# A step table in place of counted slots in the attention stage of a two-mixer step, with the multiplications of the values shared out anew

## The chip, the cores and the metric

The kernel runs on one core of one Trainium2 chip. The time is the device time of one execution in microseconds; the figure given is the median of several runs. An execution taken by the hardware profiler comes with its span (first to last instruction on the core) and with its own time, which includes what lies around the span.

Five engines work beside each other, each through its own instruction stream in order: TensorE (PE; PEld is its weight load), VectorE (DVE), ScalarE (ACT), GpSimd (POOL) and SyncE (SP, which here issues most DMAs). An instruction waits for semaphores of others, and what stands behind it on its engine waits with it. PSUM has eight banks of 128 x 512 float32.

## What is computed

One layer with two attention mixers side by side: mixer A attends to all latent tokens, mixer B to a window of 128 to each side with a sink logit; both see 128 cached context tokens. Each branch is multiplied by a SiLU gate, and both go through one output projection.

```python
h = rmsnorm(xs, norm_gain) * (1.0 + scale) + shift
q_a, k_a, v_a, g_a, q_b, k_b, v_b, g_b = project(h, w_in, ...)
...
o_a = global_attn_latent(q_a, k_a, v_a, cache_k_a, cache_v_a)
o_b = window_attn_latent(q_b, k_b, v_b, cache_k_b, cache_v_b, sink_b)
xs = xs + gate * merge_out(o_a, g_a, o_b, g_b, w_out)
...
def merge_out(o_a, g_a, o_b, g_b, w_out):
    return jnp.concatenate([o_a * jax.nn.silu(g_a), o_b * jax.nn.silu(g_b)], axis=-1) @ w_out
```

There are 1024 latent tokens (8 tiles of 128) and 128 prompt tokens (one tile, t = 0), which attend only to themselves. D is 1024; each mixer has 8 heads of 64 in 2 key/value groups. Everything is float32; matrix products are made of high and low parts (`F32R`), so that one product in the text is two or three matmuls in the code.

## The kernel before

**Stages.** To about 300 us: adaLN modulation and normalisation, then the projections (gates, queries, keys and values). Queries go to DRAM (`q_dram`, high and low halves), SiLU gates to `g_dram`, keys and values stay in SBUF. The attention stage follows, on which the change acts.

**Units and pairs.** A unit is (t, m, g): a token tile, a mixer (m = 0 is A, m = 1 is B) and a key/value group. `units` lists them tile by tile, A before B, so units 2k and 2k+1 are a pair with the same t and g. There are 18 pairs: 0 to 15 for the latent tiles, 16 and 17 for the prompt. A unit holds four heads of 128 queries.

**An A unit** (m = 0):
- `max_items`: twelve times a matmul `pmx` (L932, one head by three key blocks, a bank of tag A) and VectorE's maximum over it (L933). `finish` reduces them to `m_nat`, negated (L943, L946); `transpose` turns this 128 x 4 tile on TensorE (`ptm`, L951, a bank of tag A) and VectorE multiplies it into four rows of the query tile `qb` (L952), so that the second score matmul subtracts the maximum.
- `scores`: per key block two matmuls into `st` (L1206, L1207, a bank of tag B), ScalarE's exponential `pe` (L1208), and GpSimd's addition into `acc` (L1215), for the sums.
- `values`: per block a product into `pv` (L1228, a bank of tag C; four instructions, because the two halves of the columns go separately and each is float32), at the end one of `acc` by ones for the sums.

**A B unit** (m = 1):
- `weight_items`: per head two matmuls into `sn` (L989, L990, tag A), VectorE's masked minimum `nm` (L993), ScalarE's exponential `pen` (L979). Then small steps: GpSimd `ex` (L1011), ScalarE `sinks` (L1022), GpSimd `total` (L1025), VectorE's reciprocal `inv` (L1028). `turned` transposes `inv` (`pti`, L1040, tag A), `put` copies it (L1044) and sends it to DRAM, `rows` reads it back broadcast over partitions.
- `scores`: four transposes of `pen` into `st` (L1202, tag B) and a copy by ScalarE (L1203) per block. `values` as above.

**After the values.** For A, `inverse` makes reciprocal sums `rs` on ScalarE (L1245, L1246). GpSimd multiplies the gate tile `sgl` by the reciprocals (A at L1248, B at L1036). `gated`: VectorE multiplies `pv` by this `sgl` into `of` (L1254). `parts`: ScalarE copies it to the high part `ogh` (L1264), GpSimd subtracts for the low part `ogl` (L1267). `out_items` are the output matmuls `po` (L1305, banks D and E), 24 per pair, which fill TensorE during later pairs; VectorE adds the residual and SP stores.

**Banks.** A, B and C have two each, D and E one. A bank of a tag is used again when the readers of the one before the last are done.

**Order.** The program is written in one order, and `in_order` at the end keeps each engine to it. That order came from slots: one slot per score block, 13 for a middle pair. In each slot the loop at the end of `hybrid_step` ran `tick()` (what `later(n, f)` had put n slots ahead), one score block, the due steps (offsets MX_AT, NAT_AT, ENDS, EX_AT, ROWS_AT), six of the `late` products (the last gate columns, `late_product`, L1137) in each of the first four slots, and output matmuls at a rate of OUTRATE a slot out of a queue `outq`. Steps of the end of a unit were set relative to when its values were issued.

Of the kernel before, what the change touches and what calls it, by code (L numbers as in the profile page):

```python
# [1 line left out]

# [32 lines left out]
KS = (0, 1, 4, 5, 2, 3, 6, 7)  # L35
PL_DVE = (4,)
LAG = 2
LEAD = 4
# [4 lines left out]
NAT_AT = (0, 1, 2, 3)  # L43
NAT_FIRST = (0, 1, 2, 3)
MX_AT = (-4, -3, -2, -2, -1, 4, 5, 5, 7, 7, 8, 8)
MX_FIRST = (0, 1, 2, 3, 3, 4, 4, 5, 6, 7, 7, 8)
MX_LEAD = 3
LAST_END = (1, 3, 5, 7)
SPLIT_LAG = 2

LATE = (6, 6, 6, 6)
LATE_PUT = 9
LATE_LAG = 1
# [4 lines left out]
WO_LATE = {12: 9, 13: 10, 11: 21, 15: 21, 14: 24}  # L58

WO_STEPS = ((0, 4, 4), (1, 5, 5), (2, 6), (3, 7), (4, 8, 6), (5, 9), (6, 11), (7, 12, 10), (8, 12), (9, 13), (10, 14))  # L60
TURN = 2
QUERY_AT = (0, 2, 3, 6)
PAD = 2
# [11 lines left out]
LOADLEAD = 5  # L75
OUTRATE = 2.0
# [4 lines left out]
GATE_LATE = 2  # L81
ENDS = ((1, 3, 4), (1, 2, 3, 6))
QTS = 5
PROMPT_LEAD = 4
PROMPT_PV = "CCAC"
PROMPT_PL = ()
LOW_DVE = (-2, -1)
PROMPT_EX = (1, 2)
PROMPT_RATE = 4

HELD = 2
END_RATE = 2.5
EX_AT = (2, 2, 5)
ROWS_AT = (1, 1, 4, 6)
# [13 lines left out]
GROUP = (1, 2, 4)  # L108

# [21 lines left out]
def hybrid_step(ctx, tc, x_prompt, x_sample, cache_k_a, cache_v_a, cache_k_b, cache_v_b,  # L131
# [15 lines left out]
    agenda = {}  # L147
    now = [0]

    def later(n, f):  # L150

        agenda.setdefault(now[0] + n, []).append(f)

    def tick():
        now[0] += 1
        for f in agenda.pop(now[0], ()):
            f()
# [615 lines left out]
    with tc.tile_pool(name="kt", bufs=2) as kt:  # L773
# [94 lines left out]
        def tick_now():  # L868
            for f in agenda.pop(now[0], ()):
                f()  # L870

# [42 lines left out]

    def max_items(i):
# [4 lines left out]
        def item(h, b):  # L920
            if h == 0 and b == 0:
                mxtile[i] = qs.tile([P, 4, 3], F32, tag="mx", name=f"mx{i}", bufs=3)
            mx = mxtile[i]
            lhs = qtile[i][:, P * h : P * h + P]
# [6 lines left out]
            else:  # L931
                nc.tensor.matmul(pm[:, 0:384], lhs, kha[:, g, 3 * b : 3 * b + 3, :], start=True, stop=True)  # L932
                nc.vector.tensor_reduce(mx[:, h, b : b + 1], pm[:, 0:384], axis=AX.X, op=ALU.max)  # L933

        def finish():
# [4 lines left out]
            mn = m_nat[i // 2 % 2]  # L940
            if t > 0:
# [5 lines left out]
            later(TURN, transpose)  # L947

        def transpose():
            pt = bank("A", f"ptm{i}")  # L950
            nc.tensor.transpose(pt[0:4, 0:P].bitcast(F32R), m_nat[i // 2 % 2], ident_r)  # L951
            nc.vector.tensor_tensor(qbtile[i][64:68, :].rearrange("p (h n) -> p h n", h=4),  # L952
                                    pt[0:4, 0:P].unsqueeze(1).to_broadcast([4, 4, P]),
# [7 lines left out]
    def weight_items(i):  # L961

        t, m, g = units[i]
        v = {}

# [12 lines left out]
        def exp(h, s, scale):  # L978
            nc.scalar.activation(penat[i][:, h], s, AF.Exp, bias=v["nm"][:, h : h + 1], scale=scale,  # L979
                                 accum_out=v["sum"][:, h : h + 1])  # L980

        def item(h):
            p0, p1_ = window(t)
            n = P * (p1_ - p0)
            if h == 0:
                first(n)
# [231 lines left out]
    def values(i, made, first, last):  # L1218
# [39 lines left out]
        def parts():  # L1258
            while held[0] == NOG:
                outq.pop(0)()  # L1260
# [186 lines left out]
```

## Time and profile before

| what | value |
|---|---|
| median of 3 runs | 694.82 us (693.71 to 695.19) |
| profiled execution, own time | 694.89 us |
| its span | 693.0 us |
| mean granted TensorE clock | 0.994 |
| TensorE matmuls | 3896 |
| VectorE / ScalarE / GpSimd instructions | 857 / 692 / 340 |

The views that the next sections use: the page (busy time and share of each engine); busy time by stage, whose rows give a stretch, its length, the busy time of PE, PEld, DVE, ACT and POOL with their instruction counts, the granted clock, the DMA share and GB/s; the timeline, whose rows give the start, the duration, engine, line, operation, what is written from what, and a count where like instructions were merged, with the engine's idle time before it and who ended it in brackets; the groups of instructions by line (count, then busy us and mean ns, then idle us before and who ended it); the waits (total us, times, longest). A matmul's bar is longer than the time until the next one may start.

### The profile page before, as it was taken

How to read it: one execution, taken by the hardware profiler on the slowest of the kernel's cores; microseconds unless marked ns; L12 is line 12 of the kernel's file. 1: busy time of each engine (PE TensorE's matmuls, PEld its weight loads, DVE VectorE, ACT ScalarE, POOL GpSimd, SP SyncE). 2: the span in 40 equal slices, each digit the busy share in tenths (PEclk: the TensorE clock that was granted, in tenths of full speed). 3: DMA queues.
4: the chain of work that ended last, by engine and by line, in shares of the span. 5: the costliest groups of instructions: out<-in, count | busy, mean ns of one | idle time of the engine just before them, and what ended most of it. 6: DMA issues, size and time to landing. Idle time of an engine off the chain costs nothing.

```text
span 693.0 us, 10923 instructions
## 1 busy us (share of the span) xinstructions
PE 675.0 (97%) x3896; PEld 522.8 (75%) x3896; DVE 374.3 (54%) x857; ACT 309.0 (45%) x692; POOL 323.3 (47%) x340
## 2 busy tenths in 40 slices
PE   6999999999999999998999999999999999999997
PEld 3688988878788788985667777777777777777666
DVE  3565237875684772535446455455455563645343
ACT  4555411412243452456445445555456445545450
POOL 3466023332322140657575457545664566446730
PEclk9999999999999999999899999999999999999999
DMA  8960283339436015533122122212221212112323
GB/s 339 413 255 21 109 303 77 78 92 285 133 88 191 8 62 161 165 105 108 58 82 71 54 85 68 92 54 69 70 84 47 91 61 78 55 55 68 122 61 122
DMA packets 53446, 78.65 MB, mean 113 GB/s; under 512 B 6848, under 2 KB 25728, under 8 KB 52368
## 3 DMA queue, kind: packets, MB, share of 16 engines
q1 hardware_dynamic: 45360, 66.28, 28.4%
q10 hardware_dynamic: 8032, 11.68, 6.3%
q8 instruction: 31, 0.51, 0.3%
q14 instruction: 23, 0.19, 0.1%
HBM read 58.72 MB, written 19.21 MB: 112 GB/s over the span
## 4 chain that ended last, share of the span: by engine, by line
PE 87%; DMA 4%; DVE 3%; ACT 2%; issue 1%; POOL 1%; ACTq 1%; SPq 1%; DVEq 0%; POOLq 0%
PE pv L1228 14%; PE po L1305 14%; PE st L1206 5%; PE pmx L932 5%; PE st L1207 4%; PE pq L279 4%; PE pq L280 4%; PE pq L278 4%; PE st L1202 4%; PE pg L288 3%; PE pg L292 3%; PE pg L293 3%; PE pk L279 2%; PE pk L280 2%; PE pk L278 2%; DMA wm<-in_w_mod_ss_dram 2%
## 5 line engine op out<-in xcount | busy, mean ns | idle before, releaser
L1215 POOL TENSOR_TENSOR acc<-acc,pe 128x512 f32<-128x512 f32 x112 | 143.5, 1281 | 37.8 <-ACT pe L1208 35.4
L933 DVE TENSOR_REDUCE mx<-pmx 128x1 f32<-128x384 f32 x192 | 101.7, 554 | 103.8 <-PE pmx L932 101.5
L1208 ACT ACTIVATE pe<-st 128x512 f32<-128x512 f32 x146 | 85.4, 596 | 89.8 <-PE st L1207 89.6
L1228 PE MATMUL pv<-pe,v_all 128*64 128x256 f32 x832 | 101.6, 387 | 0.0
L1228 PEld LDWEIGHTS pv<-pe,v_all 128*64 128x64 f32 x832 | 57.3, 138 | 38.3 <-issue 8.4
L993 DVE CUSTOM_DVE_ANT_0 sn<-sn,mask,nsink 128x512 f32<-128x512 f32 (+1 forms) x64 | 46.3, 724 | 68.6 <-PE sn L990 67.9
L1305 PE MATMUL po<-wo,ogh 128*128 128x512 f32 (+1 forms) x224 | 75.8, 390 | 0.0
L197 POOL TENSOR_TENSOR rs_q<-ms_q,mhalf 128x8 f32<-128x8 f32 x18 | 34.8, 1931 | 80.8 <-DVE ms_q L195 80.8
L932 PE MATMUL pmx<-kha,qt 128*128 128x384 f32 x192 | 63.3, 376 | 3.7 <-ACT pen L979 3.1
L1215 POOL TENSOR_TENSOR acc<-pe,pe 128x512 f32<-128x512 f32 x16 | 20.4, 1276 | 96.2 <-ACT pe L1208 73.9
L1206 PE MATMUL st<-qt,kha 128*128 128x512 f32 x144 | 61.4, 426 | 1.2 <-ACT pe L1208 1.1
L979 ACT ACTIVATE pen<-sn,nm 128x512 f32<-128x512 f32 (+2 forms) x72 | 45.3, 631 | 31.4 <-DVE nm L993 28.6
L1207 PE MATMUL st<-qb,kla 68*128 68x512 f32 x144 | 57.2, 397 | 0.0
L1203 ACT COPY pe<-st 128x512 f32<-128x512 f32 x62 | 36.4, 587 | 32.9 <-PE st L1202 32.9
L932 PEld LDWEIGHTS pmx<-kha,qt 128*128 128x128 f32 x192 | 34.9, 192 | 12.8 <-ACT pen L979 7.7
L1305 PEld LDWEIGHTS po<-wo,ogh 128*128 128x128 f32 x224 | 41.5, 190 | 3.5
L1305 PE MATMUL po<-wo,ogl 128*128 128x512 f32 (+1 forms) x112 | 43.6, 389 | 0.0
L1206 PEld LDWEIGHTS st<-qt,kha 128*128 128x128 f32 x144 | 27.2, 189 | 20.9 <-issue 8.5
L1202 PE MATMUL st<-ident_r,pen 128*128 128x128 f32 x248 | 37.5, 274 | 1.1 <-DVE pen L1030 1.1
L441 POOL TENSOR_TENSOR h<-hf,h 128x256 fp32r<-128x256 f32 (+2 forms) x33 | 28.0, 862 | 20.7 <-DVE h L440 20.7
L1202 PEld LDWEIGHTS st<-ident_r,pen 128*128 128x128 f32 x248 | 29.2, 141 | 7.5 <-ACT ogh L1264 1.5
L675 ACT ACTIVATE sqq<-pq 128x512 f32<-128x512 f32 x18 | 10.8, 599 | 53.3 <-DMA qd<-qo0q 15.6
(235 smaller groups left out, 1506.9 us busy)
## 6 DMA issues: line engine op xcount, KB each, us to landing
qt<-qd SPq DMA_DIRECT2D x36, 256.0 KB
wm<-in_w_mod_ss_dram SPq DMA_DIRECT2D x8, 1024.0 KB
qd<-qo0q ACTq DMA_DIRECT2D x36, 128.0 KB
qd<-qo1q ACTq DMA_DIRECT2D x36, 128.0 KB
sgl<-gd SPq DMA_DIRECT2D x36, 128.0 KB
out_dram<-yt SPq DMA_DIRECT2D x17, 256.0 KB
xn<-in_x_sample_dram SPq DMA_DIRECT2D x8, 512.0 KB
wg<-in_w_mod_g_dram SPq DMA_DIRECT2D x4, 1024.0 KB
```

What stands on the lines that cost most here:

```text
L278: nc.tensor.matmul(out, h_at(0, i, k, tok), w.hi[k], start=(k == 0), stop=False)
L932: nc.tensor.matmul(pm[:, 0:384], lhs, kha[:, g, 3 * b : 3 * b + 3, :], start=True, stop=True)
L933: nc.vector.tensor_reduce(mx[:, h, b : b + 1], pm[:, 0:384], axis=AX.X, op=ALU.max)
L979: nc.scalar.activation(penat[i][:, h], s, AF.Exp, bias=v["nm"][:, h : h + 1], scale=scale, accum_out=v["sum"][:, h : h + 1])
L993: nc.vector.tensor_tensor_reduce(s, s, mask[:, m0 : m0 + n], -1.0, nsink[:, 4 * g + h : 4 * g + h + 1], op0=ALU.add, op1=ALU.min, accum_ou ...
L1202: nc.tensor.transpose(s[:, P * h : P * h + P], penat[i][:, h, o : o + P], ident_r.bitcast(F32))
L1206: nc.tensor.matmul(s, kh, qtile[i], start=True, stop=False)
L1207: nc.tensor.matmul(s, kl, qbtile[i], start=False, stop=True)
L1208: nc.scalar.activation(pe, s, AF.Exp)
L1215: nc.gpsimd.tensor_tensor(acc[i], first, pe, op=ALU.add)
L1228: nc.tensor.matmul(pv[HD * s : HD * s + HD, o : o + 256].rearrange("p (c n) -> p c n", c=2), lhs, r[:, :, s, :], start=start, stop=stop)
L1305: nc.tensor.matmul(po[c], x, wo_parts[KT * n + k][lo][:, q], start=(k == KS[0] and p == 0), stop=(k == KS[-1] and p == 2))
```

## The change

- All offsets of slots are replaced by a table `STEPS`: every step of a pair has a place (a real number) relative to the pair's start, pairs are `PAIR = 13` apart, and `OTHER` has places of their own for pairs 0, 15, 16 and 17. `agenda` becomes a heap, and the stage runs everything in order of its place. The places make an order only; nothing waits for a clock. Output matmuls have places too (`po`), so the queue `outq` with its rate is gone.
- The first value products of an A unit (`v1`) come after eight score blocks, before after six.
- `gated`: VectorE multiplies `pv` by the reciprocals (`rs` or `rows`), GpSimd then multiplies `of` by the gates, before the copy `ogh`. The two GpSimd multiplications of `sgl` go. The prompt's B units, whose weights are already divided, are multiplied by the gates on VectorE as before.
- `ptm` and `pti` become riders: if the next `pmx` comes within `mt_wait` or `nt_wait` steps, they are written to columns 384 to 511 of its bank, just ahead of it; otherwise to a bank of their own.
- `KS`, the order of the eight input tiles of the output matmuls, starts with the B mixer.
- The 24 late products are spread by `LATE`; loads (`qa`, `qb` query tiles, `wa`, `wb` gate tiles, `nr` rows) have places in the table.

```diff
-KS = (0, 1, 4, 5, 2, 3, 6, 7)
+KS = (4, 5, 0, 1, 6, 7, 2, 3)
...
+PAIR = 13
+STEPS = {'qa': -19.96,
+         'mx': (-16.71, -16.71, -15.16, -14.85, -13.67, -8.98, -7.88, -7.77, -6.05, -5.92, -5.82, -5.62),
+         'mf': -2.8,
+         'mt': -1.53,
+         'mt_wait': 0.01,
+         'sa': (0.08, 0.59, 1.46, 2.33, 3.28, 4.04, 6.45, 6.92, 9.09),
+         'qb': -2.9,
+         'nm': (0.23, 1.26, 1.81, 3.27),
+         'nx': (0.83, 1.26, 2.62, 3.27),
+         'nf': 3.45,
+         'ns': 4.53,
+         'nn': 5.14,
+         'nd': 6.55,
+         'nt': 7.13,
+         'nt_wait': 1.08,
+         'np': -0.21,
+         'nr': 13.0,
+         'sb': (8.81, 10.61, 11.27, 11.69),
+         'v1': 7.15,
+         'v2': 14.7,
+         'ea': 15.2,
+         'ga': 16.66,
+         'ha': 17.94,
+         'la': 19.03,
+         'gb': 16.29,
+         'hb': 17.86,
+         'lb': 18.69,
+         'po': (21.51, 22.08, 22.28, 23.38, 23.52, 23.64, 23.67, 24.08, 24.17, 24.18, 24.99, 25.69, 25.98, 26.08, 26.94, 28.37, 29.56, 29.77, 29.93, 30.27, 30.4, 31.0, 31.45, 31.48),
+         'wa': -5.73,
+         'wb': -8.28}
...
+LATE = ((-0.86, 2), (-0.61, 1), (-0.17, 3), (-0.16, 1), (1.64, 3), (2.52, 1), (2.92, 1), (2.97, 1), (3.46, 5), (5.27, 3), (5.31, 1), (6.78, 1), (6.89, 1))
...
+    def of_pair(i, name, f, k=None):
+        w = when(i, name)
+        w = PAIR * (i // 2) + (w if k is None else w[k])
+        if zero:
+            post(zero[0] + w, f)
+        else:
+            soon.append((w, f))
+
+    def beside_maxima(i, name, f, wait):
+
+        r = name, f
+        riders.append(r)
+        later(wait, lambda: r in riders and (riders.remove(r), f(bank("A", name)[0:4, 0:P])))
...
             else:
+                if riders:
+                    riders.pop(0)[1](pm[0:4, 384:512])
                 nc.tensor.matmul(pm[:, 0:384], lhs, kha[:, g, 3 * b : 3 * b + 3, :], start=True, stop=True)
...
-            later(TURN, transpose)
...
+            of_pair(i, "mt", lambda: beside_maxima(i, f"ptm{i}", transpose, when(i, "mt_wait")))
...
-            later(ROWS_AT[0], turned)
-            later(ROWS_AT[1], put)
-            later(ROWS_AT[2], rows)
-            later(ROWS_AT[3], lambda: nc.gpsimd.tensor_tensor(sgl[i], sgl[i], v["rows"], op=ALU.mult))
...
+            of_pair(i, "nt", lambda: beside_maxima(i, f"pti{i}", turned, when(i, "nt_wait")))
...
-            sg = sgl[i]
-            later(1, lambda: nc.gpsimd.tensor_tensor(sg, sg, rs.rearrange("p (c n) -> p c n", c=2), op=ALU.mult))
+            inv[i] = rs.rearrange("p (c n) -> p c n", c=2)
...
-            nc.vector.tensor_tensor(of, pv[:, 0:256].rearrange("p (c n) -> p c n", c=2), sgl.pop(i), op=ALU.mult)
-            later(GATE_LATE, lambda: load_gate(i + 4))
...
+            whole = t == 0 and m == 1
+            by = sg if whole else inv.pop(i)
+            nc.vector.tensor_tensor(of, pv[:, 0:256].rearrange("p (c n) -> p c n", c=2), by, op=ALU.mult)
+            if not whole:
+                nc.gpsimd.tensor_tensor(of, of, sg, op=ALU.mult)
             v["of"] = of
...
+        for name, f in zip("eglh", (inverse, gated, low, parts)):
+            if m == 0 or name != "e":
+                of_pair(i, name + "ab"[m], f)
         if m == 1:
-            later(ENDS[m][3], lambda: outq.extend(out_items(t, g)))
+            for k, f in enumerate(out_items(t, g)):
+                of_pair(i, "po", f, k)
...
+    while agenda:
+        n, _, f = heappop(agenda)
+        now[0] = max(now[0], n)
         f()
```

In the table a name stands for: `mx` a maximum, `mf` and `mt` the end of the maxima and ptm, `sa` and `sb` a score block of A and of B, `nm` and `nx` a head's window scores and its exponential, `nf`, `ns`, `nn`, `nd` the small steps ex, sinks, total and reciprocal, `nt`, `np`, `nr` pti, put and rows, `v1` and `v2` the value products, `e`, `g`, `h`, `l` with a or b the steps inverse, gated, parts (ogh) and low (ogl). When a step is posted after its place has passed, it runs next.

341 lines of the change are left out of this document (214 added, 127 removed).

## Prediction

> **What bounds the kernel now.** I read the page first, then the busy time by stage.
>
> ```profile
> span 693.0 us, 10923 instructions
> PE 675.0 (97%) x3896; PEld 522.8 (75%) x3896; DVE 374.3 (54%) x857; ACT 309.0 (45%) x692; POOL 323.3 (47%) x340
> ...
> 300.00:323.00 23.00, 22.56 (x138) 17.07 (x137) 8.78 (x22) 16.07 (x36) 14.94 (x14) 1.00 0.29 92
> 323.00:354.00 31.00, 27.37 (x136) 18.89 (x135) 14.94 (x35) 15.72 (x38) 20.65 (x22) 0.89 0.25 82
> 354.00:627.00 273.00, 272.87 (x1634) 200.06 (x1633) 148.00 (x337) 141.17 (x326) 159.12 (x168) 1.00 0.22 69
> 627.00:675.00 48.00, 46.02 (x292) 33.05 (x292) 20.13 (x45) 24.20 (x68) 25.98 (x33) 1.00 0.29 88
> ```
>
> TensorE sets the time. The change acts only after 300 us, in the attention stage, and removes no matmul; so it can gain only what TensorE loses there to waits and to a lower clock (third number from the right). The busy column hides short waits, since a matmul's bar is longer than its share of the pipe. The distance from one start to the next shows them. TensorE's timeline in a middle pair:
>
> ```profile
> 432.08 0.60 PE L1202 MATMUL st<-ident_r,pen 128*128 128x128 f32 x4
> 432.44 0.60 PE L932 MATMUL pmx<-kha,qt 128*128 128x384 f32 x2
> 432.87 0.39 PE L1305 MATMUL po<-wo,ogl 128*128 128x512 f32 x1
> 433.10 0.40 PE L1305 MATMUL po<-wo,ogh 128*128 128x512 f32 x1
> 433.51 0.22 PE L951 MATMUL ptm<-ident_r,m_nat 128*4 128x128 f32 x1
> ...
> 438.07 0.60 PE L1228 MATMUL pv<-acc,ones 128*64 128x256 f32 x4
> 438.51 1.68 PE L1228 MATMUL pv<-pe,v_all 128*64 128x256 f32 x14
> ...
> 444.33 0.39 PE L1206 MATMUL st<-qt,kha 128*128 128x512 f32 x1
> 444.56 0.39 PE L1207 MATMUL st<-qb,kla 68*128 68x512 f32 x1
> 444.82 0.62 PE L932 MATMUL pmx<-kha,qt 128*128 128x384 f32 x2
> 445.28 0.39 PE L1305 MATMUL po<-wo_big,ogh 128*128 128x512 f32 x1
> ...
> L951 PE MATMUL ptm<-ident_r,m_nat x12: 223/224/227, 365.2 to 615.6; 128*4 128x128 f32 x12
> PEld ptm L951 <- DVE mx L933: 5.3, 12, 0.5
> PEld pmx L932 <- ACT pen L979: 3.3, 11, 0.3
> ```
>
> A 512-column matmul costs 0.23 us (432.87 to 433.10, 444.33 to 444.56). Four transposes and two maxima take 432.08 to 432.87, 0.79: I take 0.11 a transpose and 0.175 a maximum. A value product (four instructions) takes 0.44 to the next start; I use 0.43. A pair of units issues 24 output, 18 score and 8 window matmuls (50 x 0.23 = 11.5), 12 maxima (2.1), 16+2 transposes (2.0) and 14 value products (6.0): 21.6, and a few tenths where value products begin and end. The pairs are 22.76 apart (twelve ptm from 365.2 to 615.6, 250.4 / 11). So the middle is nearly full: at most a few tenths per pair can go.
>
> Two of them have names. Ahead of ptm the last output matmul lasts 433.10 to 433.51, 0.41 instead of 0.23: 0.18, twelve times, ended by a VectorE maximum that frees one of the two A banks. Ahead of the maxima at 444.82 stand 0.26 instead of 0.23, and the two take 0.46 instead of 0.35: 0.14, eleven times, ended by ScalarE's exponential of pen, which holds the other bank.
>
> The large holes lie at the stage's start and end:
>
> ```profile
> 323.75 0.39 PE L1207 MATMUL st<-qb,kla 68*128 68x512 f32 x1
> 324.47 0.44 PE L932 MATMUL pmx<-kha,qt 128*128 128x384 f32 x1 [0.33 <-ACT pen L979]
> ...
> 325.30 0.40 PE L1207 MATMUL st<-qb,kla 68*128 68x512 f32 x1
> 327.08 1.01 PE L932 MATMUL pmx<-kha,qt 128*128 128x384 f32 x2 [1.38 <-ACT pen L979]
> ...
> 351.55 0.39 PE L1207 MATMUL st<-qb,kla 68*128 68x512 f32 x1
> 353.32 0.61 PE L932 MATMUL pmx<-kha,qt 128*128 128x384 f32 x2 [1.38 <-ACT pen L979]
> ...
> 665.96 0.27 PE L1003 MATMUL sn<-klp,qt 128*128 128x128 f32 x1
> ...
> 668.52 0.63 PE L1228 MATMUL pv<-pe,v_all 128*64 128x256 f32 x4
> 670.21 0.63 PE L1202 MATMUL st<-ident_r,pen 128*128 128x128 f32 x4 [1.06 <-DVE pen L1030]
> ```
>
> What made the hole at 327.08 stands in the timeline of all engines, and the clock behind it in two-microsecond windows:
>
> ```profile
> 325.23 0.73 POOL L1248 TENSOR_TENSOR sgl<-sgl,rs 128x256 f32<-128x256 f32 x1
> 325.30 0.42 DVE L1254 TENSOR_TENSOR spare<-pv,sgl 128x256 f32<-128x256 f32 x1 [1.59 <-POOL sgl L1036]
> 325.64 0.62 DVE L993 CUSTOM_DVE_ANT_0 sn<-sn,mask,nsink 128x384 f32<-128x384 f32 x1
> 325.76 0.41 ACT L1264 CAST ogh<-spare 128x256 fp32r<-128x256 f32 x1 [0.86 <-DVE spare L1254]
> ...
> 326.00:328.00 2.00, 0.92 (x3) 0.92 (x4) 1.26 (x5) 1.81 (x6) 1.52 (x2) 0.71 0.32 98
> 328.00:330.00 2.00, 2.00 (x7) 1.57 (x6) 0.83 (x2) 1.17 (x4) 2.00 (x4) 0.50 0.94 295
> 330.00:332.00 2.00, 2.00 (x8) 1.09 (x8) 1.02 (x2) 0.43 (x1) 2.00 (x4) 0.50 0.55 196
> 332.00:334.00 2.00, 2.00 (x14) 1.12 (x12) 0.00 (x0) 0.00 (x0) 1.92 (x2) 0.59 0.06 22
> ```
>
> VectorE stood 1.59 us before L1254 because GpSimd had not yet multiplied the gates; behind it in VectorE's queue stood the window minimum (L993), behind that ScalarE's copy ogh and the exponential of pen, and that exponential holds the A bank which TensorE needs. Then the clock was halved to about 333 us.
>
> **The change, part by part.** *The multiplications.* VectorE now multiplies pv by reciprocal sums, GpSimd the product by the gates. Counts and sizes stay (per pair two of 0.42 on VectorE, two of 0.75 on GpSimd), but VectorE no longer waits for GpSimd, and the C bank is free a GpSimd product earlier. GpSimd moves between VectorE and the copy ogh, so now ScalarE waits for it: everything behind ogh in ScalarE's queue (exponentials of the next scores) is late when GpSimd is. The table answers by putting ogh 1.28 to 1.57 steps behind the multiplication; a step is 22.76 / 13 = 1.75 us. Is that enough? Durations:
>
> ```profile
> L1215 POOL TENSOR_TENSOR acc<-acc,pe 128x512 f32<-128x512 f32 x112 | 143.5, 1281 | 37.8 <-ACT pe L1208 35.4
> L1208 ACT ACTIVATE pe<-st 128x512 f32<-128x512 f32 x146 | 85.4, 596 | 89.8 <-PE st L1207 89.6
> L1248 POOL TENSOR_TENSOR sgl<-sgl,rs 128x256 f32<-128x256 f32 x18 | 13.4, 746 | 5.3 <-ACT rs L1246 3.9 <-PE pv L1228 1.4
> ```
>
> I sort a middle pair's steps and lay TensorE's work end to end by the costs above, from the output matmul before its first scores: window scores nm3 end at 7.2, score block 4 at 7.7, block 7 at 11.4, the first value products (now eight blocks, before six) run from 11.9 to 15.3. Window minimum and exponential (0.76 + 0.14, then 0.69) put the last pen at 9.0, the exponential of block 4 (0.60) at 9.6. GpSimd adds block 4 until 10.95, multiplies the b unit until 11.7, makes ex (0.2), multiplies the a unit until 12.65. ScalarE, which has nothing ready from 10.2, copies ogh to 13.05, then exponentiates blocks 6 and 7 by 13.65 and 14.25. The value products need them at 14.4 and 14.9. So ScalarE's new wait, 2 us, is covered by the six blocks ahead, with 0.6 to spare: **no TensorE time** in the middle pairs, and **the two 1.38 us holes go**: 1.78 - 0.23 and 1.77 - 0.23, **3.1**.
>
> *The clock.* The windows miss 2 x (0.29 + 0.50 + 0.50 + 0.41) = 3.4 us of clock; part of the first fell into the hole, so I take **2.9** as lost and let it go with the hole. [...]
>
> *Small transposes.* Where a maximum is due within its wait, ptm and pti go into columns 384 to 511 of its bank, otherwise they take a bank as before. In the table's middle pairs pti rides on maximum 10, behind the value products; ptm, with a wait of 0.01 step, still takes its own, but now four transposes and two output matmuls (0.9 us) stand between it and the last maximum, against the maximum's 0.55 on VectorE. So the 0.18 goes: x 12 = **2.1**. The first maximum behind nm3 now has score block 4 and three output matmuls ahead (0.46 + 0.69) and comes at 8.4, when the pen it needs ended at 8.0: the 0.14 goes, x 11 = **1.5**; the slack there is the smallest, 0.3.
>
> *The start.* Unit 0's ptm moves to the head of the stage; seven late products (7 x 0.175 = 1.2) cover VectorE's multiplication behind it. The late products, before six a step, now lie one to five at a time between scores. In the second pair no output matmul exists yet as filler; laid out the same way, its score block 6 and the maxima ahead of it wait 1.3 us for ScalarE. Before, that pair lost 324.47 - 323.75 - 0.23 = 0.5 beside its hole. Net **0.8 lost**.
>
> *The end.* 670.21 - 668.52 - 0.43 - 0.1 (end of the value products) = **1.2** went to the prompt's chain of small steps, which took 4.2 us from the last prompt scores (665.96) to the transposes of its weights (670.21). In the new order 7 us of matmuls lie between the two (value products of pairs 15 and 16, eight output matmuls, scores), so it goes.
>
> *At nothing:* the order of the eight output products KS (the b halves first, which are ready first); loads at other times. SP's queue is in order: a qt load at +6.04 steps waits in some pairs for a buffer whose last score is at +9.09, 3 steps or 5 us, and the gate loads and output stores behind it wait with it; they are needed over 5 steps later. The rows of reciprocals are issued 3.3 steps, 5.8 us, ahead of VectorE's use; were they late, VectorE would stand, and maxima behind it.
>
> *New waits.* The layout shows none in the middle, but it is laid to 0.3 and 0.6 us, and something I don't see may bind. From below 0; from above as much as each of sixteen pairs loses now, 0.18 + 0.14, 5.1 in all. Nearest to the layout I take 0.05 a pair, **0.8 lost**.
>
> Sum: 3.1 + 2.9 + 2.1 + 1.5 - 0.8 + 1.2 - 0.8 = 9.2. The profiled execution took 694.89 (span 693.03 and 1.86 around it), and the median is 694.82, so it serves for both: 694.9 - 9.2 = **685.7**.
>
> **Rivals.** *The clock falls all the same* (for: the second pair still has no filler and a laid wait of 1.3, and an equal hole at 353 us is followed by a clock of 1.00, so the hole alone doesn't decide; against: no slow window elsewhere after 300 us). 685.7 + 2.9 = 688.6.
>
> *Slower: GpSimd stands in ScalarE's way.* Place: ogh behind the a unit's multiplication. The cover is 0.6. If GpSimd is later than laid by d, each of 14 pairs loses d - 0.6; it eats the 9.2 at d = 0.6 + 9.2 / 14 = 1.26, just one more accumulate (1.28) ahead of the multiplication. At d = 2.0: 14 x 1.4 = 19.6, 685.7 + 19.6 = 705. For: GpSimd is 58% busy in the middle (159 of 273) and its accumulates themselves wait for ScalarE, a loop. Against: the layout has the accumulates in the table's order already.
>
> *Not what it says:* the holes move to other banks; 694.9.
>
> **How the numbers follow.** Forecast 0.68 (681 to 688.6), the clock falls all the same 0.14 (688.6, to 692), no change 0.05 (694.9), slower 0.13 (705). The range's low end: no new wait, no 1.3 in the second pair, and a further 2.7 for the few tenths a pair (0.2 x 14) that the sum of 21.6 leaves unexplained: 685.7 - 0.8 - 1.3 - 2.7 = 681. Its high end: the clock rival with most of the 5.1 of new waits, 692. It leaves out the last two cases, 0.18. About 0.2% (1.4 us) is what a measurement of this kernel can tell from no change. Faster 0.82, same 0.05, slower 0.13.
>
> **What would show it.** Right: no VectorE wait ended by GpSimd before the pv multiplication; no wait ahead of ptm; pairs 22.4 apart; clock 1.00 from 326 to 334; ogh waiting 1 to 2 us for GpSimd without a TensorE hole behind. Wrong: TensorE waiting for L1208 at score 6 or 7 in every pair (GpSimd too late), a slow window in the second pair, or pairs still 22.8 apart.

## The result and the profile after

| what | before | after |
|---|---|---|
| median | 694.27 us (692.18 to 695.19, 4 runs) | 686.88 us (685.83 to 688.53, 4 runs) |
| after / before | | 0.990, 95% interval 0.9869 to 0.9931 |
| profiled execution, own time | 694.89 us | 688.53 us (the longest of its four) |
| its span and mean granted clock | 693.0 us, 0.994 | 686.7 us, 0.997 |

The changed kernel is faster by 1.0%, 7.4 us in the medians, where 9.2 was forecast, and 1.2 us above the forecast of 685.7. That the total came so near hides that the forecast missed the parts: the middle went the other way, and the start and the end missed by 0.7 and 1.4. The runs below take them apart. Line numbers differ from the kernel before: `st` is L1371 and L1372, `pe` L1373, `pmx` L1078, `pen` L1132, `ptm` L1100, `pv` L1393, VectorE's multiplication L1423, GpSimd's L1425, `ogh` L1431, the load of `qb` L1083, the residual's load `yt` L1453, the load of the rows L1211, ScalarE's `sinks` (written to `ex`) L1174, the store of the late gate columns `gd` L1312.

The page of the changed kernel, span and busy time by engine:

```profile
span 686.7 us, 10946 instructions
PE 666.8 (97%) x3896; PEld 524.1 (76%) x3896; DVE 377.7 (55%) x857; ACT 308.9 (45%) x692; POOL 323.3 (47%) x340
```

The same work, and again a TensorE that hardly ever is idle by this line. Busy time by stage, with the columns as before:

```profile
323.00:354.00 31.00, 29.05 (x167) 20.79 (x168) 16.70 (x38) 17.15 (x40) 22.24 (x25) 0.94 0.31 91
354.00:627.00 273.00, 267.57 (x1632) 201.81 (x1630) 150.73 (x335) 141.73 (x324) 158.21 (x168) 1.00 0.22 69
627.00:675.00 48.00, 48.00 (x301) 36.13 (x298) 22.83 (x49) 23.05 (x66) 25.67 (x32) 1.00 0.31 102
```

Three readings. The stretch 323 to 354 improved (27.37 busy at a clock of 0.89 before) but still has a hole and a low clock. The end is full (46.02 before). The middle, which the forecast wanted 2.8 us shorter, has lost busy time: 272.87 before, 267.57 now. TensorE's waits say to what; its weight loads' waits have the row that answers to ptm's of before; and the distance of the pairs says how much:

```profile
PE st L1372 <- DMA qb<-qd: 5.2, 6, 1.2
...
PE pmx L1078 <- ACT pen L1132: 1.9, 1, 1.9
```

```profile
PEld ptm L1100 <- DVE mx L1079: 0.7, 1, 0.7
```

```profile
L1100 PE MATMUL ptm<-ident_r,m_nat x12: 304/305/305, 360.3 to 611.9; 128*4 128x128 f32 x12
```

The twelve waits ahead of ptm (5.3 us) are one, of 0.7. But a wait that did not exist before stands at the head: six times the second score matmul waits for its query tile `qb` to land. The pairs are (611.9 - 360.3) / 11 = 22.87 apart, against 22.76 before.

From these ptm the spans split into three parts. The stage's head is marked by the second ptm before (300.2; the first, of unit 0, stood at 285.8) and by the first after (299.8), with the same work behind them: 1619 and 1618 matmuls. The marks of the fourth pair and of the last of the twelve also part the same matmuls in both kernels, to within one.

| stretch | before | after | difference | forecast |
|---|---|---|---|---|
| head of the stage to the ptm of the fourth pair | 65.0 | 60.5 | -4.5 | -5.2 |
| middle, eleven pairs | 250.4 | 251.6 | +1.2 | -2.8 |
| from there to the end of the span | 77.4 | 74.8 | -2.6 | -1.2 |

With 0.4 less ahead of the head of the stage this makes the 6.3 us between the spans. The forecast column sorts the prediction's terms: holes 3.1, clock 2.9 and 0.8 lost in the second pair; ptm 2.1, maxima 1.5 and 0.8 of new waits; the prompt's chain 1.2.

**The middle.** The timeline of TensorE in one of the six pairs, and SyncE's issues ahead of it:

```profile
589.89 0.40 PE L1371 MATMUL st<-qt,kha 128*128 128x512 f32 x1
591.50 0.47 PE L1372 MATMUL st<-qb,kla 68*128 68x512 f32 x1 [1.21 <-DMA qb<-qd]
```

```profile
584.74 0.37 SPq L1352 DMA_DIRECT2D sgl<-gd  x1
585.17 0.93 SPq L1453 DMA_DIRECT2D yt<-in_x_sample_dram  x2
586.14 0.44 SPq L1035 DMA_DIRECT2D qt<-qd  x1
586.68 0.47 SPq L1083 DMA_DIRECT2D qb<-qd  x1
```

The qb load (128 KB) is the last of five issued within 2 us: 128 KB of gates, two residual tiles and a query tile of 256 KB each stand ahead of it, 1 MB with its own. The DMA engines were 97% busy from 586 to 588:

```profile
586.00:588.00 2.00, 2.00 (x14) 1.74 (x13) 1.91 (x6) 0.59 (x1) 1.09 (x1) 1.00 0.97 304
```

At 304 GB/s, 1.05 MB take 3.4 us, the whole lead that qb has; the matmul that needs qb starts 4.8 us after the issue, 591.50 - 589.89 - 0.23 = 1.4 us late. These 1.4 lie beyond what the bytes alone take, and I did not follow them. Residual tiles are loaded in every second pair (a token tile has two pairs), and it is every second pair that waits. By the distances of the starts the six lose 0.6 to 1.4 each, 6.2 us together. Before, SyncE issued the residual's loads some 10 us ahead of qb (490.30 and 500.15 in one pair), now 1.5 us.

**The second pair.** The timeline of all engines, around the place where the hole of 1.38 us was:

```profile
318.91 0.33 SPq L1312 DMA_DIRECT2D gd<-spare  x1
319.34 2.48 SPq L1211 DMA_DIRECT2D spare<-rd  x2
...
323.41 0.39 PE L1372 MATMUL st<-qb,kla 68*128 68x512 f32 x1
323.96 0.42 DVE L1423 TENSOR_TENSOR spare<-pv,spare 128x256 f32<-128x256 f32 x1 [3.95 <-DMA spare<-rd]
...
325.01 0.58 ACT L1132 ACTIVATE pen<-sn,nm 128x384 f32<-128x384 f32 x1 [1.38 <-DVE nm L1147]
...
325.74 0.44 PE L1078 MATMUL pmx<-kha,qt 128*128 128x384 f32 x1 [1.94 <-ACT pen L1132]
```

The chain has the links of before (VectorE stands ahead of its multiplication, behind it stand the window minimum, the exponential pen, and the maximum that wants the A bank), with another head: not GpSimd's gates but the rows of reciprocals of pair 0, issued at 319.34 (the second of the two only by 321.82) and landed only at 323.9. No bytes stood in their way: the DMA engines were 13 to 26% busy from 318 to 324 us. What stood ahead of them in SyncE's queue is the store of the late gate columns (L1312), which waited 4.9 us, until 318.91, for VectorE's product L1311 (318.33 to 318.88). The clock behind the hole:

```profile
326.00:328.00 2.00, 1.98 (x8) 1.36 (x8) 1.58 (x3) 1.27 (x4) 1.55 (x2) 0.80 0.81 235
328.00:330.00 2.00, 2.00 (x9) 1.18 (x9) 0.00 (x0) 1.19 (x4) 2.00 (x4) 0.50 0.92 203
330.00:332.00 2.00, 2.00 (x18) 1.29 (x16) 1.09 (x3) 0.71 (x2) 2.00 (x5) 0.84 0.79 267
```

It misses 2 x (0.20 + 0.50 + 0.16) = 1.7 us here, against 3.4 before.

**What the forecast feared, in the middle.** The same view, GpSimd, ScalarE and TensorE in a middle pair, behind the two multiplications:

```profile
511.47 0.73 POOL L1425 TENSOR_TENSOR spare<-spare,sgl 128x256 f32<-128x256 f32 x1
511.48 3.67 PE L1393 MATMUL pv<-pe,v_all 128*64 128x256 f32 x32
511.56 0.20 ACT L1174 ACTIVATE ex<-ex 128x4 f32<-128x4 f32 x1 [1.83 <-POOL ex L1167]
...
512.24 0.41 ACT L1431 CAST ogh<-spare 128x256 fp32r<-128x256 f32 x1 [0.18 <-POOL spare L1425]
512.55 1.08 ACT L1373 ACTIVATE pe<-st 128x512 f32<-128x512 f32 x2
```

ScalarE waits 2.0 us for GpSimd, as much as was laid out, but 1.83 of it at the small step `ex` (L1174), which GpSimd makes between its two multiplications, and only 0.18 at the second ogh. The exponentials of blocks 6 and 7 run behind, until about 513.1 and 513.63. TensorE wants them at 511.48 + 6 x 0.43 = 514.1 and 514.5. The cover is 0.9 us; I had laid 0.6. No TensorE time is lost here.

### The profile page after: what moved, and what is told of

The parts are those of the page before. It is cut to its first block, busy times and chain, and to the rows that moved or that the text cites. A ratio compares the mean times of both kernels' runs of the same rounds, so it can differ in the third digit from the quotient of the medians.

```text
span 686.7 us, 10946 instructions
## 1 busy us (share of the span) xinstructions
PE 666.8 (97%) x3896; PEld 524.1 (76%) x3896; DVE 377.7 (55%) x857; ACT 308.9 (45%) x692; POOL 323.3 (47%) x340
## 4 chain that ended last, share of the span: by engine, by line
PE 86%; DMA 8%; DVE 3%; issue 1%; ACT 1%; ACTq 1%; SPq 0%; DVEq 0%
PE pv L1393 14%; PE po L1478 13%; PE st L1372 5%; PE st L1371 5%; PE pmx L1078 4%; PE pq L406 4%; PE pq L407 4%; PE pq L405 4%; DMA qb<-qd 4%; PE pg L415 3%; PE pg L420 3%; PE pg L419 3%; PE st L1366 3%; PE sn L1143 2%; PE pk L406 2%; PE pk L407 2%
## 5 line engine op out<-in xcount | busy, mean ns | idle before, releaser
L1079 DVE TENSOR_REDUCE mx<-pmx 128x1 f32<-128x384 f32 x192 | 100.0, 551 | 55.2 <-PE pmx L1078 54.4
L1373 ACT ACTIVATE pe<-st 128x512 f32<-128x512 f32 x146 | 83.4, 594 | 47.9 <-PE st L1372 46.3
L1393 PE MATMUL pv<-pe,v_all 128*64 128x256 f32 x832 | 100.9, 385 | 0.0
L1393 PEld LDWEIGHTS pv<-pe,v_all 128*64 128x64 f32 x832 | 57.0, 137 | 36.0 <-issue 6.5
L1478 PE MATMUL po<-wo,ogh 128*128 128x512 f32 (+1 forms) x224 | 81.5, 396 | 0.0
L1372 PE MATMUL st<-qb,kla 68*128 68x512 f32 x144 | 57.9, 402 | 5.2 <-DMA qb<-qd 5.2
L1078 PE MATMUL pmx<-kha,qt 128*128 128x384 f32 x192 | 57.9, 349 | 2.5 <-ACT pen L1132 1.9
L1371 PE MATMUL st<-qt,kha 128*128 128x512 f32 x144 | 57.4, 398 | 0.0
L1132 ACT ACTIVATE pen<-sn,nm 128x512 f32<-128x512 f32 (+2 forms) x72 | 45.0, 627 | 16.5 <-DVE nm L1147 13.3
L1078 PEld LDWEIGHTS pmx<-kha,qt 128*128 128x128 f32 x192 | 35.3, 190 | 8.9 <-ACT pen L1132 2.5
L1372 PEld LDWEIGHTS st<-qb,kla 68*128 68x128 f32 x144 | 27.2, 189 | 12.8 <-DVE po L1481 5.1
L1366 PE MATMUL st<-ident_r,pen 128*128 128x128 f32 x248 | 36.1, 273 | 0.0
```

Of the source, the lines that this page charges most:

```text
L1366: nc.tensor.transpose(s[:, P * h : P * h + P], penat[i][:, h, o : o + P], ident_r.bitcast(F32))
L1371: nc.tensor.matmul(s, kh, qtile[i], start=True, stop=False)
L1372: nc.tensor.matmul(s, kl, qbtile[i], start=False, stop=True)
L1373: nc.scalar.activation(pe, s, AF.Exp)
L1393: nc.tensor.matmul(pv[HD * s : HD * s + HD, o : o + 256].rearrange("p (c n) -> p c n", c=2), lhs, r[:, :, s, :], start=start, stop=stop)
L1478: nc.tensor.matmul(po[c], x, wo_parts[KT * n + k][lo][:, q], start=(k == KS[0] and p == 0), stop=(k == KS[-1] and p == 2))
```

## The experiments

The theory after the result: the holes, ptm and the maxima gave what was forecast, and two DMAs that land late (qb in six pairs, rows in the second pair) took part of it back. Rivals: the pairs are longer for another reason and the named waits only stand where the time shows; the exchange of the multiplications alone brings the gain; the sharing of banks brings nothing. Each job had its own runs of the kernel before beside it: medians of 693.15 (9 runs; the first three edits and the exchanged multiplications in the old slots), 693.56 (15 runs; the changed kernel again and the three behind it) and 693.53 (7 runs; banks of their own and the repeat of both edits). Beside the first result stood 694.27 (4 runs), so a difference between the changed kernel's 686.88 and a run of another job is good to about 1 us.

### The query rows earlier

The load of qb is taken out of `finish` and placed 8 steps ahead of the pair (`finish` stands at -2.8):

```diff
-            qb_ = qp.tile([68, 512], F32R, tag="qb", name=f"qb{i}", bufs=2)
-            nc.sync.dma_start(qb_[0:64, :].bitcast(F32), ...)
-            qbtile[i] = qb_
+            if i not in qbtile:
+                load_qb()
...
+        if i not in EARLY:
+            post(zero[0] + PAIR * (i // 2) - QB_AT, load_qb)      # QB_AT = 8.0
```

> The changed kernel with the load of qb moved from its place with the last maxima (-2.8 steps) to -8 steps, nothing else. In the changed kernel's trace the second score matmul of every other middle pair waits 0.3 to 1.4 us for this load (TensorE waits 5.2 us in six such places, some 6 us with the slower matmul behind each). Theory (the load is late because it is issued behind two residual loads and a query load of 256 KB each, which go only with every other pair): those waits vanish, and the kernel is 5 to 7 us faster than the changed one, 680 to 682 us. Rival (TensorE would wait at that place for VectorE's rows of qb, or the middle is bound elsewhere): the load lands earlier and the time moves by under 1.5 us.

Measured 682.06 us (680.40 to 683.55, 4 runs), 0.9841 of the kernel before (0.9821 to 0.9862): 4.8 below the changed kernel's 686.88, 4.1 to 4.9 by the ratios to the kernel before (0.9900 and, in its repetition, 0.9912), just short of the 5 to 7 expected. No wait for qb is left in TensorE's list; what heads its waits in this stage is the second pair's hole, and the pairs are closer (ptm is L1108, pmx L1079 and pen L1140 here):

```profile
PE pmx L1079 <- ACT pen L1140: 2.3, 1, 2.3
```

```profile
L1108 PE MATMUL ptm<-ident_r,m_nat x12: 304/305/305, 360.8 to 607.1; 128*4 128x128 f32 x12
```

The twelve ptm run over 246.3 us, 4.1 less than before the change and 5.3 less than with it. So the late qb load made the middle longer, and the rival of another reason falls; without it the middle gives more than the 2.8 of the forecast. The four times fall in two groups, 680.4 and 680.8 with a mean granted clock of 1.000, 683.3 and 683.6 with 0.997.

### The rows of pair 0 earlier

```diff
-             'nr': 14.8,
+             'nr': 11.0,
```

> The changed kernel with the place of the first pair's rows load alone moved from 14.8 to 11.0 steps. In the changed kernel VectorE waits 4 us for these rows at 324 us, TensorE has a hole of 1.9 us there, and the clock is at half from about 327 to 331 us. Theory (the hole comes from the late rows, and the low clock from the hole): VectorE's wait and the hole go, the clock stays at 1.00, and the kernel is 3.5 to 4.5 us faster than the changed one, 682 to 684 us. Rival 1 (the clock falls for lack of work in the second pair, hole or no hole): hole gone, low clock still there, 1.5 to 2.5 us faster. Rival 2 (another step holds the same place): under 1 us.

Measured 685.97 us (685.33 to 686.38, 4 runs), 0.9898 (0.9884 to 0.9911). The stretch of the second pair, and the maximum behind pen:

```profile
323.00:354.00 31.00, 30.31 (x185) 21.89 (x185) 18.21 (x40) 17.54 (x42) 24.48 (x28) 1.00 0.30 90
```

```profile
324.24 0.44 PE L1078 MATMUL pmx<-kha,qt 128*128 128x384 f32 x1 [0.45 <-ACT pen L1132]
```

At 11.0 the rows stand ahead of the store of the gate columns, and SyncE issues them at 314.77. In the profiled execution the hole's cause is confirmed: with the rows in time it shrinks from 1.94 to 0.45, and the clock stays at 1.00; the first ptm and that of the fourth pair are 357.7 - 299.8 = 57.9 apart, against 60.5. But the median gains only 0.9 us on the changed kernel's 686.88, 0.1 to 1.0 by the ratios, which is not clear of the noise. The expected 3.5 to 4.5 was missed; by size it is the second rival (under 1 us), though the trace shows hole and slow clock gone. The mean clock of the changed kernel's own executions ran from 0.997 to 0.999, so not all of them lost what the profiled one did; how much of the hole the others had can't be seen without their traces.

### Both

> Both moves together: qb loaded at -8 steps and the first pair's rows at 11.0. If the two places are independent the gains add: 9 to 11 us below the changed kernel, 676 to 678 us. If the qb waits take up what the rows free, less than 8 us.

Measured 681.33 us (679.87 to 681.50, 5 runs), 0.9826 (0.9813 to 0.9840), and once more, unaltered, in the last job:

> The kernel with the earlier query rows and the earlier rows of pair 0, unaltered, as the measure beside the kernel with banks of their own: 680 to 683 by both theories.

681.34 us (680.71 to 682.41, 4 runs), 0.9824 (0.9809 to 0.9838). Eight of these nine executions had a clock of 0.998 or more, one 0.996 (682.41, the longest). The twelve ptm of the first:

```profile
L1108 PE MATMUL ptm<-ident_r,m_nat x12: 304/305/305, 358.0 to 605.0; 128*4 128x128 f32 x12
```

(605.0 - 358.0) / 11 = 22.45 a pair, with 1.2 us of waits for query tiles in two of them. This is the best version. The two edits give 5.5 together, as their parts do (4.8 and 0.9); what fell is the larger sum that I had worked out from the profiled execution's hole and clock. On the executions of the first experiment at clock 1.000 (680.4, 680.8) the earlier rows gain nothing; what they can take away is executions like the two at 683.

### The exchanged multiplications in the old slots

The kernel before, with VectorE multiplying by the reciprocals and GpSimd by the gates, the copy ogh one slot behind as it was:

```diff
-            later(1, lambda: nc.gpsimd.tensor_tensor(sg, sg, rs..., op=ALU.mult))
+            inv[i] = rs.rearrange("p (c n) -> p c n", c=2)
...
-            nc.vector.tensor_tensor(of, pv..., sgl.pop(i), op=ALU.mult)
+            by = sg if whole else inv.pop(i)
+            nc.vector.tensor_tensor(of, pv..., by, op=ALU.mult)
+            if not whole:
+                nc.gpsimd.tensor_tensor(of, of, sg, op=ALU.mult)
```

> The kernel before with its slots, and of the change only the multiplications: VectorE multiplies pv by the reciprocals, GpSimd the product by the gates, the copy ogh one slot behind as it was. Theory of the prediction (the two holes of 1.38 us came from VectorE behind GpSimd): VectorE's wait for GpSimd goes, but with ogh only one slot (1.75 us) behind, ScalarE now waits for GpSimd instead, up to 2 us a pair, without the cover that the new order gives; so the holes change place and the time lies between 690 and 700 us. Rival (the multiplications are what made the change faster): 686 to 689 us, without the table.

Measured 703.45 us (702.82 to 704.07, 4 runs), 1.0151 (1.0137 to 1.0165): 10.3 slower than the kernel before, and beyond the 690 to 700 expected. The timeline of a middle pair (L1257 is GpSimd's multiplication, L1267 ogh, L1207 pe), and TensorE's list:

```profile
447.84 0.41 ACT L1267 CAST ogh<-spare 128x256 fp32r<-128x256 f32 x1 [0.50 <-POOL spare L1257]
...
448.80 0.50 PE L1205 MATMUL st<-qt,kha 128*128 128x512 f32 x1 [0.35 <-ACT pe L1207]
```

```profile
PE st L1205 <- ACT pe L1207: 5.7, 15, 0.6
```

```profile
L951 PE MATMUL ptm<-ident_r,m_nat x11: 223/227/227, 364.7 to 600.3; 128*4 128x128 f32 x11
```

Eleven ptm over 235.6 us make 23.56 a pair, 0.8 more than before. This is the "slower" rival, at its place: ScalarE waits for GpSimd ahead of ogh, the exponential behind it is late, and a score matmul finds no B bank. The wait for pe takes nearly half of the 0.8; the rest lies in shorter waits that I did not follow. The exchange alone costs time.

### The changed kernel again

> The changed kernel again, unaltered, as the measure for the runs beside it. The moves of e1 and e3 together gave 681.3 us. In the changed kernel's own runs the time lay between 685.8 and 688.5 with the clock between 0.999 and 0.997; if the hole in the second pair lowers the clock in some executions and not in others, its runs lie in two groups some 2 to 3 us apart, while e3's, which have no such hole, lie within 1.7 us. If not, one group with a median of 686 to 687 us.

687.29 us (685.93 to 688.46, 5 runs), 0.9912 (0.9894 to 0.9929). The two groups that I thought possible do not show: the five times are spread over 2.5 us, all with a mean clock of 0.996 to 0.998. It is the measure for the next three, which ran beside it.

### The old multiplication in the new table

The changed kernel, with GpSimd multiplying the gates by the reciprocals first and VectorE waiting for it, at the places `ga` and `gb`:

```diff
-            nc.vector.tensor_tensor(of, pv..., by, op=ALU.mult)
-            if not whole:
-                nc.gpsimd.tensor_tensor(of, of, sg, op=ALU.mult)
+            if not whole:
+                nc.gpsimd.tensor_tensor(sg, sg, by, op=ALU.mult)
+            nc.vector.tensor_tensor(of, pv..., sg, op=ALU.mult)
```

> The changed kernel with the multiplications in the old roles at the new places: GpSimd multiplies the gates by the reciprocals, VectorE then pv by that. Theory: VectorE stands behind GpSimd again (its product comes after the addition of score block 4), and behind VectorE's multiplication stand the maxima that free the A banks; by the layout GpSimd is done 3 to 4 us after VectorE is ready, maximum 7 waits for maximum 5, and TensorE loses 2 to 3 us in each of 14 pairs: 715 to 730 us. Rival (the table's places leave room for either order): under 3 us slower than the changed kernel.

Measured 766.26 us (765.59 to 768.94, 4 runs), 1.1059 (1.1038 to 1.1081): 79 us above the changed kernel, the right sign and far beyond the size that I gave it. The timeline of one pair, the waits, and the clock there:

```profile
440.89 0.42 DVE L1425 TENSOR_TENSOR spare<-pv,sgl 128x256 f32<-128x256 f32 x1 [3.43 <-POOL sgl L1424]
...
442.67 0.69 PE L1078 MATMUL pmx<-kha,qt 128*128 128x384 f32 x1 [3.52 <-DVE mx L1079]
```

```profile
PE pmx L1078 <- DVE mx L1079: 47.5, 15, 3.5
```

```profile
442.00:444.00 2.00, 1.33 (x3) 1.15 (x4) 1.64 (x4) 0.41 (x1) 2.00 (x4) 0.50 0.22 66
```

VectorE stands 3.4 us for GpSimd, with the maxima behind it, so TensorE stands 3.5 us in nearly every pair (47.5 us), and the clock is at half already while TensorE stands: it is 0.50 in the window from 442 to 444, and the hole shown lasts until 442.67. Its mean over the span is 0.957, which is 0.043 x 763.8 = 33 us. 47.5 + 33 = 80 is an estimate of the price: the waits' rows show less than the waits cost (5.2 for 6.2 at qb), and some of the slow clock falls into the holes, where it costs nothing. Neither half of the change pays by itself: the exchange needs the table's cover, and the table with these places needs the exchange. Whether other places would suit the old multiplication was not tried.

### ptm back where the maximum is not yet done

```diff
-         'mt': -1.53,
+         'mt': -1.84,
```

> The changed kernel with ptm of the middle pairs put directly behind maximum 3 (-1.84 steps for -1.53), without the four transposes and two output matmuls between. Theory (ptm costs what it waits for the bank of the last maximum but one): in the trace maximum 2 starts at 519.35 and its reduction ends at 520.28, while ptm would be ready at 519.93, so 0.35 us a pair, thirteen times: 4 to 5 us slower than the changed kernel. Rival (the wait was for the tile m_nat itself, or later waits take it up): under 1.5 us.

Measured 691.73 us (689.54 to 693.06, 11 runs), 0.9972 (0.9961 to 0.9983): 4.4 above the changed kernel in the same job, as expected (4 to 5). TensorE's list:

```profile
PE ptm L1100 <- DVE mx L1079: 4.7, 14, 1.0
```

A third of a step in ptm's place brings back a wait in 14 pairs. The 4.4 is a net figure: by the distances of the starts ptm loses 0.40 in each of the pairs, while qb's waits, with more time to land, fall from 6.2 to 3.5 us. The gain that the forecast put down to ptm comes from its place; ptm still takes a bank of its own (all 18 do, in the changed kernel).

### GpSimd made late on purpose

Three products of 128x256 (2.0 us together) whose result is not used, ahead of the a unit's multiplication by the gates. They overwrite reciprocals that have been used:

```diff
             if not whole:
+                if m == 0 and t:
+                    for _ in range(3):
+                        nc.gpsimd.tensor_tensor(by, by, by, op=ALU.mult)
                 nc.gpsimd.tensor_tensor(of, of, sg, op=ALU.mult)
```

> The changed kernel with GpSimd made late: three more products of 128x256 on GpSimd (0.74 us each, 2.2 in all; results unused) ahead of the A unit's multiplication by the gates, in every latent pair. The prediction's slower rival: the cover is 0.6 us and each pair loses the rest, 14 x 1.6 = 22 us, 709 us. By the changed kernel's trace the last exponential ends 1.0 us before the value products need it, so 14 x 1.2 = 17 us, 704 us. Rival (GpSimd's lateness is hidden elsewhere, ScalarE has slack): under 5 us.

Measured 707.12 us (706.98 to 707.88, 4 runs), 1.0201 (1.0187 to 1.0215): 19.8 above the changed kernel. The timeline (L1428 is GpSimd's multiplication, L1434 ogh):

```profile
450.29 0.41 ACT L1434 CAST ogh<-spare 128x256 fp32r<-128x256 f32 x1 [2.14 <-POOL spare L1428]
...
451.24 1.14 PE L1393 MATMUL pv<-pe,v_all 128*64 128x256 f32 x8 [0.86 <-ACT pe L1373]
```

ogh's wait grew from 0.18 to 2.14, so GpSimd is 1.96 later. The products of block 6 start 1.24 behind those of block 5 instead of 0.21, 1.03 lost at this place (the row shows 0.86), so 0.9 us were covered, as read from the trace of the changed kernel; the layout had 0.6. The total, 707.1, lies between the 709 and the 704 worked out ahead. It is 19.8 for sixteen pairs, 1.2 each; where the rest beyond 1.03 is lost I did not follow. The value products wait for pe, the place that the slower rival named.

### Banks of their own again

The version with both edits, and the sharing taken back. pti and ptm stand at the same place in TensorE's order, but in a bank of tag A of their own:

```diff
+            if t and riders:
+                name, f = riders.pop(0)
+                f(bank("A", name)[0:4, 0:P])
             pm = bank("A", f"pmx{i}_{h}_{b}")
...
-                if riders:
-                    riders.pop(0)[1](pm[0:4, 384:512])
```

> The kernel with the earlier query rows and the earlier rows of pair 0 (681.3), with one thing taken back: pti and ptm stand at the same place in TensorE's order, but in a bank of their own, ahead of the maximum on which they rode. Theory, the sharing is worth time: in the middle pairs pti stands ahead of two maxima that follow each other by 0.175 us; in a bank of its own it takes one of the two A banks, and the second of these maxima has to wait until ScalarE has copied pti (transpose 0.27, copy 0.26, and up to 0.6 for an exponential in ScalarE's way). I lay 0.5 a pair for 14 pairs, 7 us: 688, with waits of that maximum for ScalarE in TensorE's list, 0.3 to 0.9 each. Rival, the sharing is worth nothing in this order because the A banks have slack there: within 1.5 us of the same kernel with the sharing (680 to 683), and no new wait.

Measured 686.38 us (684.63 to 686.89, 4 runs), 0.9890 (0.9871 to 0.9909): 5.0 above the same kernel with the sharing; 7 was laid. TensorE's timeline behind the value products, first with the sharing (the repeated run), then without:

```profile
442.80 0.27 PE L1203 MATMUL pmx<-ident_r,inv 128*4 128x128 f32 x1
442.82 0.60 PE L1079 MATMUL pmx<-kha,qt 128*128 128x384 f32 x2
443.26 0.39 PE L1486 MATMUL po<-wo,ogh 128*128 128x512 f32 x1
```

```profile
443.40 0.27 PE L1204 MATMUL pti<-ident_r,inv 128*4 128x128 f32 x1
443.42 0.42 PE L1080 MATMUL pmx<-kha,qt 128*128 128x384 f32 x1
444.01 0.44 PE L1080 MATMUL pmx<-kha,qt 128*128 128x384 f32 x1 [0.17 <-ACT spare L1212]
444.29 0.39 PE L1487 MATMUL po<-wo,ogh 128*128 128x512 f32 x1
```

With the sharing the next output matmul starts 0.44 after the first maximum, without it 0.87: the second maximum waits until ScalarE has copied pti (L1212). 0.43 x 14 = 6.0, of which 5.0 reach the end. The list of waits shows only 2.4 of it, since a matmul's bar covers part of such a wait. The sharing is worth time at pti, in this order.

## Why the prediction came out, step by step

- **The holes (3.1)**: right for their cause. VectorE no longer waits for GpSimd ahead of the multiplication, and the hole at 353 us is gone. The one at 327 us came back, 1.94 us long, with the rows' DMA at its head.
- **The clock (2.9)**: the rival "the clock falls all the same" held in the profiled execution, with 1.7 instead of 3.4 us missing, and with another head of the hole than the rival had in mind. The term was taken from an execution with a mean clock of 0.994. Of 31 later executions of the kernel before, 7 had 1.000 (691.9 to 692.5 us), 23 had 0.996 to 0.998 (693.1 to 694.1) and one 0.994 (694.7), so the typical loss was less than 2.9 and so was what could be won. Which holes a low clock followed, and for how long, is told under the hardware, below.
- **ptm (2.1)** and **the maxima (1.5)**: right in kind: neither wait stands in the lists any more, and moving ptm back brings its wait back. Their sizes were not measured one by one. Together, less 0.8 of new waits, they are 2.8; the middle with the query rows earlier gives 4.1, that is 1.3 more; its pairs are 246.3 / 11 = 22.39 apart, the forecast said 22.4.
- **The second pair (0.8 lost)**: taken with the holes and the clock, the start gave 4.5 of 5.2, the late rows included. With the rows in time it gave 65.0 - 57.9 = 7.1: the wait of 1.3 us that I laid there measured 0.45 by its row, 0.6 by the starts.
- **The end (1.2)**: right in kind, too small. It gave 2.6, and TensorE's busy time from 627 to 675 us is the whole 48.00. The rest is a second hole of the kernel before, which the prediction did not see: 648.15 - 646.90 - 0.23 = 1.0 us ahead of a score matmul that waited for ScalarE, with 0.2 more at the next one. None of it is left.

```profile
648.15 0.50 PE L1206 MATMUL st<-qt,kha 128*128 128x512 f32 x1 [0.86 <-ACT pe L1208]
```

- **The banks**: I counted the sharing of pti as nothing. Against the kernel before that is nearly so, since pti there stood between single maxima; but the new order, with two maxima behind pti, would lose 5.0 without it. The prediction weighed the parts against the old order only.
- **At nothing: loads at other times.** This is the step that failed. It asked how far ahead each load was issued (rows 5.8 us, gate loads and stores over 5 steps) and found that enough. It did not list what stands ahead of each load in SyncE's queue: the bytes issued just before it, and the issues that wait. qb, not named there at all, is issued 3.4 us ahead (586.68 for 590.12 in the pair shown), behind 0.9 MB, and landed 0.6 to 1.4 late in six pairs: 6.2 us. The rows of pair 0, the case that the prediction named ("were they late, VectorE would stand, and maxima behind it"), landed late as described: pair 0 has places of its own in the table, where its rows stand behind the store of the late gate columns, and this store held SyncE for 4.9 us. So they are issued 2.7 us ahead of the place where VectorE would have used them (319.34 to 322.01, the start of that multiplication with the rows earlier), not 5.8.
- **The slower rival** did not come, for the reason given: cover. It was 0.9 instead of 0.6. The 2 us that ScalarE was to wait for GpSimd came too, but nearly all of it at `ex` and not at ogh. The exchange in the old slots and GpSimd made late show the rival's price, without the table's cover and beyond it.

So the forecast's 9.2 stood at about 6.3 between the profiled spans: 4.0 short in the middle, 0.7 short at the start, 1.4 over at the end, and 0.4 ahead of the stage, on which the change does not act. The median lies nearer to the forecast than that, in part because the profiled execution of the changed kernel was its longest of four. That the total came within 1.2 us is partly luck: an unforeseen loss of 6.2 at qb stood against gains in the middle and at the end that were larger than forecast. The order KS, the later first value products and the spread of the late products were never varied alone; their shares stay open.

## What to carry to other kernels

When a schedule moves loads, list for each load what the same queue issues in the few microseconds ahead of it and divide the bytes by the rate seen: a lead of 3.4 us was too short behind 0.9 MB, though the DMA engines were 22% busy in that stage. Ask too whether an issue ahead of it waits: a store that waited 4.9 us held two small loads back while the DMA engines were at most 26% busy. When the operand that an engine waits for is exchanged, ask which engine waits now and what cover stands behind it; the same two lines of code were worth 79 us in one order and cost 10 in the other. Weigh a part of a change inside the new order as well as against the old one.

## What the hardware showed

**The length of a hole alone did not decide whether the clock fell.** The second pair's hole in two more executions, the changed kernel repeated (first the matmul behind the hole, then the clock):

```profile
325.50 0.69 PE L1078 MATMUL pmx<-kha,qt 128*128 128x384 f32 x1 [1.79 <-ACT pen L1132]
```

```profile
325.00:327.00 2.00, 1.50 (x4) 1.31 (x5) 1.11 (x4) 1.50 (x5) 1.54 (x2) 0.62 0.39 106
327.00:329.00 2.00, 2.00 (x7) 1.71 (x6) 1.02 (x2) 1.02 (x3) 2.00 (x4) 0.53 0.91 253
```

and the experiment with ptm moved back:

```profile
325.86 0.44 PE L1078 MATMUL pmx<-kha,qt 128*128 128x384 f32 x1 [1.85 <-ACT pen L1132]
```

```profile
327.00:329.00 2.00, 2.00 (x11) 1.50 (x13) 1.01 (x2) 0.61 (x2) 2.00 (x3) 1.00 1.00 235
```

A hole of 1.79 us was followed by half the clock, and so were those of 1.94 (the changed kernel, 0.50 from 328 to 330) and of 2.33 (the query rows earlier, 0.50 from 327 to 330). One of 1.85 at the same place was not, nor was one of 1.98 (GpSimd made late): in both the windows from 325 to 332 have a clock of 1.00. In the old multiplication in the new table the low clock was there before the hole had ended: TensorE stood from 442.67 - 3.52 = 439.15 to 442.67, and the window from 442 to 444 has 0.50. What decides, these runs do not show.

**The time at half clock behind the second pair's hole was 3.4 us or 6.8.** The windows miss 1.7 us in the changed kernel's profiled execution and in the repeated one (2 x (0.38 + 0.47)), 3.4 in the kernel before. At half clock that is a stretch of 3.4 us in the first two and of 6.8 in the third. Why it was these lengths was not shown.

**A wait's row showed less than the wait cost.** 2.4 us in the list of waits stood for 5.0 us of time (banks of their own), and 5.2 for 6.2 (qb); the distance from start to start is what to add up.
